# Attention: when ScalarE's and GpSimd's extra work is issued, and in what pieces

## The chip, the cores and the metric

One Trainium2 chip, one core of it. The metric is the device time of the whole program in microseconds (us). The kernel before took 2564.64 us (median of 3 runs, 2563.76 to 2566.25). The times below that name a place in the program are microseconds from the start of the span of one profiled execution.

## The reference

One layer of an encoder: 2048 tokens, width 1024, 16 heads of 64. The mixer has two kinds of heads. Eight are stick-breaking heads: for a query t, the weight of key s < t is sigmoid(z_s) times the product of (1 - sigmoid(z)) over the keys between s and t. Eight are chunk heads: a softmax over the own chunk of 64 keys and the 8 chunks before it, with a learned bias. The heads' outputs are joined, projected, and added to the input; a squared-ReLU MLP of width 4096 follows.

```python
log_beta = jax.nn.log_sigmoid(z)
log_1m_beta = jnp.where(strict, jax.nn.log_sigmoid(-z), 0.0)
suffix = lax.cumsum(log_1m_beta, axis=3, reverse=True) - log_1m_beta
w = jnp.where(strict, jnp.exp(log_beta + suffix), 0.0)
outs.append(jnp.einsum('bhqk,bkhd->bqhd', w.astype(v.dtype), vb))
```

All is float32. The kernel holds each float32 operand as a high and a low half and multiplies them in two or three matmuls.

## The kernel before

**Stages.** The projections fill the first 415 us, the attention 415 to 1262 us, the rest of the output projection and the MLP the time from there on. Each engine works through its instructions in the order in which the program issues them, so the order in which the code below calls `act`, `pool`, `dve` and `pe` is the order of the work. A helper records every operation, and that is why all compute rows of the trace carry the line L42; the rows are told apart by the names of their tiles.

**Units and steps.** The attention is cut into units: a head `h`, a group `g` of 512 queries (taken from the end of the sequence), and for a stick-breaking (SB) unit a block `c` of 512 keys. The units come in four runs: 24 SB units, 24 chunk (CA) units, 56 SB units, 8 CA units. Where one run ends and the next begins, the kind of heads changes; the text calls this a turn, and there are three. Each unit has 4 steps, so there are 448 steps in 847 us, 1.89 us each. The main loop does in step `i` the front half of unit step `i` and the back half of unit step `i - 8`:

- TensorE (PE) transposes the weights of the back unit into PSUM (tile `wt`);
- front half, `soft1` and `soft2`: for SB, ScalarE (ACT) takes the sigmoid of the scores `z`, VectorE (DVE) scans the products into `p`, GpSimd (POOL) copies one column of `p` and subtracts neighbours into the weights `b`; for CA, DVE adds the bias (`s`), ACT takes the exponential `e`, POOL divides (`e<-e,cols`);
- `parts`: ACT casts the high half of the transposed weights (`wth<-wt`), DVE subtracts the low half (`wtl<-wt,wth`);
- the jobs in `done`, which are the extra work;
- PE multiplies the weights with the values into the accumulator (`acc`), three `wt` tiles behind;
- PE computes the scores of the next step (`z`, or `cz` and `ct` for CA);
- `fill`: PE takes matmuls of the dense queue (tiles `pf`, `po`), as many as a credit allows. A dense row that ends sets `rest`, and `fill` then issues no dense work for that step.

The scores and the transposed weights share 4 PSUM buffers: `z`, `cz`, `ct` and `wt` of a step can be written only when DVE or ACT has read the tile that held the buffer. `acc` has 2 buffers.

**The extra work.** Jobs that one step puts in `soon` run in the next step's `done`, all of them. When a unit ends, `finish` copies the two 64-row halves of its accumulator on ACT (`otmp<-acc`, `o<-acc`) in one step. After the second head of a pair, `total` adds the two on POOL in the next step (`o<-o,otmp`, 128x512), and two steps on `keep` splits the sum: a cast on ACT (`os<-o`), a subtraction on POOL (`os<-o,os`), and a store to `scr_m`, from SP's queue. The RMS norm of finished rows runs beside this: ACT squares a row (`sq<-xr`), POOL adds it up (`r<-r,sq`, 128x512). A finished dense row of the projections also brings an ACT cast (`stf<-pf`, `svf<-pf`). At a turn, ACT loads another table for the new function, and does it by a 1-column activation (`cols<-zero`), before `parts`.

Of the kernel before, what the change touches and what calls it, by code (L numbers as in the profile page):

```python
# [9 lines left out]
F32 = mybir.dt.float32  # L10
F32R = mybir.dt.float32r
BF16 = mybir.dt.bfloat16
AF = mybir.ActivationFunctionType
# [66 lines left out]
def encoder_kernel(ctx, tc, xT, x3, wf, c, g1, g2, w_in, w_rest, gqk, bias, w_o, w1, w2, w_ada, b_ada, out):  # L80
# [670 lines left out]
    if True:  # L751
# [36 lines left out]
        def finish(u):  # L788
            r = (u.h % 2) * HD
            q = HD - r  # L790
            if u.h % 2 == 0:
                pend["o", u.g] = [op.tile([P, TB], F32, tag=t, name=f"{t}{u.nm}", bufs=3) for t in ("o", "otmp")]
            o, tmp = pend["o", u.g]
            act.copy(tmp[r : r + HD, :], u.acc[q : q + HD, :])
            act.copy(o[r : r + HD, :], u.acc[r : r + HD, :])
            if u.h % 2:
                soon.append(lambda: total(u, o, tmp))

        def total(u, o, tmp):

            pool.tensor_tensor(o, o, tmp, op=ALU.add)
            soon.append(lambda: soon.append(lambda: keep(u, o)))

        def keep(u, o):

            os = fp.tile([P, 2, TB], F32R, tag="st", name=f"os{u.nm}")
            split(os[:, 0, :], os[:, 1, :], o, pool)
            q = act if u is units[-1] else sp
            q.dma_start(scr_m[u.g, u.ca * 4 + u.h // 2], os.bitcast(F32))
            pairs[u.g] += 1  # L810
            if pairs[u.g] == KT and u.g > 0:
                filler.append(Filler(outproj, u.g))
# [4 lines left out]
        class Unit:  # L817
# [24 lines left out]

            def values(self, j):
                if j == 0 and self.first:
                    pend["acc"] = ppo.tile([P, TB], F32, tag="acc", name=f"acc{self.nm}")
                self.acc = pend["acc"]
                w = self.wt.pop(j)
                end = self.last and j == len(self.banks) - 1
                for m, (kb, q0, q1, at) in enumerate(self.banks[j]):
                    mine = slice(at * P, (at + q1 - q0) * P)  # L850
                    for l in range(2):
                        pe.matmul(
                            self.acc[:, q0 * P : q1 * P], self.v[kb // 4][:, kb % 4, :], w[l][:, mine],
                            start=self.first and j + m + l == 0, stop=end and l == 1 and m == len(self.banks[j]) - 1,
                        )
                if end:
                    soon.append(lambda: finish(self))

        DIAG = [[(3, 0, 4, 0)], [(2, 0, 3, 0), (0, 0, 1, 3)], [(1, 0, 2, 0)]]

# [313 lines left out]
        def finish_row(g, n, ps, xr):  # L1174

            residual(g, n, ps, xr)
            if g < 2 and drain:
                return
            stores.pop()()
            if g < 2:  # L1180
                return

            def square():
                sq = rows[g] if n == 0 else op.tile([P, TB], F32, tag="otmp", name=f"sq{g}_{n}", bufs=3)
                act.activation(sq, xr, AF.Square)
                if n:
                    soon.append(lambda: add(sq))

            def add(sq):
                pool.tensor_tensor(rows[g], rows[g], sq, op=ALU.add)  # L1190
                if n == KT - 1:
                    later.add(3, second)

            def second():
                pv = norm_sum(dense, rows[g], f"m{g}")

                def mean():
                    v = norm_mean(op, pv, f"m{g}")
                    y = op.tile([P, 4], F32, tag="ny", name=f"nym{g}")
                    rsqrt(y, v, op.tile([P, 4], F32, tag="nt", name=f"ntm{g}"))  # L1200
                    later.add(3, lambda: spread(y))

                later.add(2, mean)

            def spread(y):
                dg = norm_diag(op, y, f"m{g}")
                later.add(2, lambda: third(dg))
# [9 lines left out]
            soon.append(square)  # L1217

        LAG = 8
        STEPS = 4  # L1220
# [12 lines left out]
        credit = 0.0  # L1233
        rest = 0
        late, soon, first, second = [], [], [], []

        def fill(part, more=0):
# [31 lines left out]
        def load(u):  # L1269
            nonlocal kp1  # L1270
            if u.ca and u.g == 0 and u.h == 0:
                narrow.close()
                kp1 = narrow.enter_context(tc.tile_pool(name="kp2", bufs=3, side="right"))
            need = (10, 11) if u.ca else (2, 3, 0, 1) + ((4, 5) if u.g == 0 else ())
            if u.g < 2:
                while not all((p, u.g) in have for p in need):
                    later.flush()
                    for job in soon:
# [30 lines left out]
        for i in range(len(steps) + LAG):  # L1309
            if i % STEPS == 0:  # L1310
                if i // STEPS + AHEAD < len(units):
                    load(units[i // STEPS + AHEAD])
            vi = i - VST
            if vi >= 0 and vi % STEPS == 0 and vi // STEPS < len(units):
                units[vi // STEPS].load_values()
            front, fs = steps[i] if i < len(steps) else (None, 0)
            back, bs = steps[i - LAG] if i >= LAG else (None, 0)
            done = list(soon)
            soon.clear()
            js = []  # L1320
# [12 lines left out]
            if turned:  # L1333
                act.activation(cols[:, 1:2], zero, AF.Exp if front.ca else AF.Sigmoid)
            for j in js:
                back.parts(j)
                late.append((back, j))
            if turned:
                front.soft1(fs)
            if front is not None:  # L1340
                front.soft2(fs)
            for job in done:
                if turned:
                    later.add(3, job)
                else:
                    job()
            while len(late) > AVLAG:
                value(*late.pop(0))
            if i + 1 < len(steps):
                u, st = steps[i + 1]  # L1350
                u.scores(st)
            fill(front.weight if front else 0.6, 6 if turned else 0)
            if i + 1 < len(steps):
                u.behind(st)
            later.tick()
        for u, j in late:
            value(u, j)
        while soon:
            soon.pop(0)()
        later.flush()  # L1360
        while second:
            second.pop(0)()
    sp = osp
# [525 lines left out]
```

## Time and profile before

| what | value |
|---|---|
| median of 3 runs | 2564.64 us |
| the profiled execution | 2562.64 us |
| its span, first to last instruction | 2560.9 us |
| PE busy over the span | 2548.6 us |
| attention stage, 415 to 1262 us | 847.0 us |
| PE, PEld, DVE, ACT, POOL busy in that stage | 843.6, 742.2, 728.8, 604.6, 569.0 us |
| granted TensorE clock | 1.000 |

The profiled execution is 1.7 us longer than its span and 2.0 us shorter than the median of the runs. PE is TensorE's matmuls, and PEld is its weight loads, each of which runs ahead of its matmul. A row of the timeline reads: start, duration, engine, line, operation, out<-in, shape, count, and in brackets the idle time before it with what ended that idle time. In a list of waits, a row reads: engine and tile that waited, what it waited for, the us in total, how many times, and the longest.

### The profile page before, as it was taken

The page shows a single profiled execution, that of the slowest core. Times are in us where ns is not written, and L with a number is a line of the kernel's source. Part 1 is how long each engine was busy: PE and PEld are TensorE (multiplying, and loading weights), DVE is VectorE, ACT ScalarE, POOL GpSimd, SP SyncE. Part 2 cuts the span into 40 slices and gives each one's busy share as a digit, 9 for nine tenths or more (in the row PEclk, how much of TensorE's full clock was granted, in tenths as well). Part 3 has the DMA queues.
Part 4 walks back from the last instruction along what each step waited for, and adds up shares of the span by engine and source line. Part 5 has one row for each costly group of instructions (what it writes and reads, how often), then busy time and mean ns, then how long its engine had stood idle before and what let it go on. Part 6 is the DMA issues. An engine that isn't in the chain of part 4 may idle for free.

```text
span 2560.9 us, 39227 instructions
## 1 busy us (share of the span) xinstructions
PE 2548.6 (100%) x12851; PEld 2153.9 (84%) x12851; DVE 1866.3 (73%) x3102; ACT 1396.2 (55%) x2599; POOL 903.4 (35%) x1232
## 2 busy tenths in 40 slices
PE   9999999999999999999999999999999999999999
PEld 7888888889999988888888888888888888888887
DVE  7656767887779999998687787768756655555655
ACT  7323434778886666666654444656444444444443
POOL 4330244766667666776423333000003233100000
PEclk9999999999999999999999999999999999999999
DMA  9879887788888685757787777966773444465574
GB/s 396 337 282 373 314 325 253 247 270 269 252 254 271 214 268 196 239 187 226 249 335 259 256 264 277 338 225 218 255 247 135 154 154 144 164 241 192 202 272 151
DMA packets 251264, 633.90 MB, mean 248 GB/s; under 512 B 28210, under 2 KB 56882, under 8 KB 241203
## 3 DMA queue, kind: packets, MB, share of 16 engines
q1 hardware_dynamic: 249760, 626.67, 70.8%
q10 hardware_dynamic: 1298, 4.72, 0.5%
q8 instruction: 101, 1.65, 0.3%
q14 instruction: 105, 0.85, 0.1%
HBM read 439.92 MB, written 191.37 MB: 247 GB/s over the span
## 4 chain that ended last, share of the span: by engine, by line
PE 92%; DVE 3%; ACT 1%; DMA 1%; issue 1%; POOL 1%; SPq 0%; DVEq 0%; ACTq 0%; POOLq 0%
PE ps L42 46%; PE pt L42 11%; PE acc L42 7%; PE wt L42 7%; PE pf L42 6%; PE z L42 5%; PE po L42 4%; PE pq L42 3%; PE cz L42 2%; PE ct L42 1%; DVE p L42 1%; DVE h L42 1%; PE px L42 1%; POOL b L42 0%; DVE cy L42 0%
## 5 line engine op out<-in xcount | busy, mean ns | idle before, releaser
L42 PE MATMUL ps<-oph,opv 128*128 128x512 f32 x2688 | 611.9, 389 | 0.1
L42 PE MATMUL ps<-h,opw 128*128 128x512 f32 x2664 | 604.2, 389 | 0.0
L42 PEld LDWEIGHTS ps<-oph,opv 128*128 128x128 f32 x2688 | 503.9, 188 | 106.1 <-DVE opv L42 0.8
L42 PEld LDWEIGHTS ps<-h,opw 128*128 128x128 f32 x2664 | 500.0, 188 | 103.8
L42 POOL TENSOR_TENSOR b<-p 128x512 f32<-128x512 f32 (+1 forms) x320 | 292.4, 914 | 201.0 <-DVE p L42 121.5
L42 ACT CAST wth<-wt 128x512 fp32r<-128x512 f32 (+1 forms) x432 | 244.2, 567 | 167.2 <-PE wt L42 162.4
L42 DVE TENSOR_TENSOR wtl<-wt,wth 128x512 fp32r<-128x512 f32 (+1 forms) x432 | 279.9, 652 | 61.8 <-ACT wth L42 60.3
L42 DVE TENSOR_TENSOR oph<-hw,oph 128x512 fp32r<-128x512 f32 x224 | 156.1, 697 | 211.5 <-ACT oph L42 211.4
L42 ACT CAST oph<-hw 128x512 fp32r<-128x512 f32 x224 | 139.4, 622 | 274.9 <-PE ps L42 272.9
L42 PE MATMUL pt<-w,ht 128*128 128x512 f32 x1248 | 288.0, 391 | 0.0
L42 POOL TENSOR_TENSOR ts<-w 128x512 f32<-128x512 f32 x32 | 45.2, 1414 | 662.2 <-DMA w<-in_w_dram 516.8
L42 PEld LDWEIGHTS pt<-w,ht 128*128 128x128 f32 x1248 | 233.0, 188 | 47.5
L42 DVE TENSOR_TENSOR_SCAN p<-z,p,zero 128x512 f32<-128x512 f32 x192 | 245.5, 1280 | 30.8 <-ACT z L42 20.3
L42 PE MATMUL acc<-wth,v 128*128 128x512 f32 (+3 forms) x544 | 217.3, 404 | 0.0
L42 ACT ACTIVATE z<-z 128x512 f32<-128x512 f32 (+1 forms) x320 | 165.8, 520 | 61.9 <-PE z L42 58.0
L42 PE MATMUL z<-k,q 128*128 128x512 f32 (+3 forms) x640 | 183.5, 368 | 2.1 <-DVE p L42 1.7
L42 PE MATMUL acc<-wtl,v 128*128 128x512 f32 (+3 forms) x544 | 181.1, 347 | 0.0
L42 DVE TENSOR_TENSOR opw<-w,opw 128x512 fp32r<-128x512 f32 x127 | 96.4, 761 | 113.2 <-ACT opw L42 113.1
L42 POOL TENSOR_TENSOR e<-e,cols 128x640 f32<-128x640 f32 (+1 forms) x128 | 143.2, 1122 | 84.6 <-DVE cols L42 66.0
L42 PE MATMUL wt<-ident,b 128*128 128x128 f32 x1088 | 165.9, 272 | 0.7 <-DVE cols L42 0.3
L42 PE MATMUL po<-fx,ow 128*128 128x512 f32 x576 | 162.0, 393 | 0.0
L42 DVE TENSOR_TENSOR opv<-hw,opv 128x512 fp32r<-128x512 f32 x224 | 155.8, 695 | 0.0
(201 smaller groups left out, 4061.0 us busy)
## 6 DMA issues: line engine op xcount, KB each, us to landing
hw<-scr_hid SPq DMA_DIRECT2D x112, 512.0 KB, 3.8
q<-scr_q SPq DMA_DIRECT2D x128, 256.0 KB, 4.7
w<-in_w_dram SPq DMA_DIRECT2D x64, 512.0 KB, 5.4
hw<-scr_s SPq DMA_DIRECT2D x64, 512.0 KB, 4.6
fw<-scr_w SPq DMA_DIRECT2D x28, 1024.0 KB, 6.9
k<-scr_k SPq DMA_DIRECT2D x224, 128.0 KB, 4.2
v<-scr_v SPq DMA_DIRECT2D x112, 256.0 KB, 4.2
wa<-in_w_ada_dram SPq DMA_DIRECT2D x48, 512.0 KB, 7.7
```

Of the source, the lines that this page charges most:

```text
L42: return lambda *x, **y: self.tc.keep_in_program_order(f(*x, **y))
```

## The change

The extra work goes into two queues, `acts` for ACT and `pools` for POOL. At the end of a step's front half one job is taken from each; after a turn none is taken for that step and the two that follow; a step that has jobs in `done` takes none from `acts` unless an accumulator is waiting to be copied; in the last 8 steps, where no front unit is left, all are taken at once. An accumulator's second copy is put at the head of `acts` when the first is issued. The POOL additions and subtractions of 128x512 are cut in two of 128x256. The cast `os` comes 3 steps after the second half of its addition (1 in the last steps). A list `full` holds the units whose accumulators are not yet copied; before a new accumulator and before `parts`, copies are forced until at most one is left. The table load of a turn is issued one step earlier in the program. The stores to `scr_m` of the last steps go by ACT's queue. The norm's reciprocal root and its diagonal are cut over steps, and `fill` clears `rest` at a turn.

The first place is ACT's order where an SB unit ends shortly before the third turn (`otmp` and `o` are the two halves of its accumulator, `z` a sigmoid, `wth` a cast of `parts`, `sq` a square of the norm). Before:

```order
L42 CAST wth_7_0_1_0_15005<-wt_7_0_1_0_14994 128x512
L42 COPY otmp_6_0_3_15010<-acc_6_0_0_14599 64x512
L42 COPY o_6_0_3_15009<-acc_6_0_0_14599 64x512
L42 ACTIVATE z_7_0_3_1_15016<-z_7_0_3_1_15016 128x512
L42 CAST wth_7_0_1_1_15032<-wt_7_0_1_1_15021 128x512
L42 ACTIVATE z_7_0_3_2_15042<-z_7_0_3_2_15042 128x512
L42 CAST wth_7_0_1_2_15068<-wt_7_0_1_2_15057 128x512
L42 ACTIVATE sq_7_15072<-xr_7_14568 128x512
L42 ACTIVATE z_7_0_3_3_15076<-z_7_0_3_3_15076 128x512
L42 CAST wth_7_0_1_3_15101<-wt_7_0_1_3_15090 128x512
L42 ACT_TABLE_LOAD
```

Now:

```order
L42 CAST wth_7_0_1_0_15073<-wt_7_0_1_0_15062 128x512
L42 COPY otmp_6_0_3_15078<-acc_6_0_0_14661 64x512
L42 ACTIVATE z_7_0_3_1_15083<-z_7_0_3_1_15083 128x512
L42 CAST wth_7_0_1_1_15099<-wt_7_0_1_1_15088 128x512
L42 COPY o_6_0_3_15077<-acc_6_0_0_14661 64x512
L42 ACTIVATE z_7_0_3_2_15110<-z_7_0_3_2_15110 128x512
L42 CAST wth_7_0_1_2_15136<-wt_7_0_1_2_15125 128x512
L42 ACTIVATE sq_7_15140<-xr_7_14632 128x512
L42 ACTIVATE z_7_0_3_3_15144<-z_7_0_3_3_15144 128x512
L42 ACT_TABLE_LOAD
L42 ACTIVATE cols<-zero 128x1
L42 CAST wth_7_0_1_3_15170<-wt_7_0_1_3_15158 128x512
```

The second copy of the accumulator has moved behind one sigmoid and one cast, and the table load has moved ahead of one cast.

The second place is POOL's order around the end of the pair of heads 0 and 1 in the last query group of the second SB run (`b` is a weight, `p` its scan, `r` the sum of squares, `o` the pair's sum, `os` its low half). Before:

```order
L42 TENSOR_TENSOR r_11570<-r_11570,sq_6_12972 128x512
L42 TENSOR_TENSOR o_0_0_3_12569<-o_0_0_3_12569,otmp_0_0_3_12570 128x512
L42 COPY p_2_0_3_2_13020<-p_2_0_2_2_12903 128x1
L42 TENSOR_TENSOR b_2_0_3_2_13019<-p_2_0_3_2_13020 128x512
L42 COPY p_2_0_3_3_13042<-p_2_0_2_3_12921 128x1
L42 TENSOR_TENSOR b_2_0_3_3_13041<-p_2_0_3_3_13042 128x512
L42 TENSOR_TENSOR os_1_0_3_13051<-o_0_0_3_12569,os_1_0_3_13051 128x512
```

Now:

```order
L42 TENSOR_TENSOR r_11612<-r_11612,sq_6_13025 128x256
L42 COPY p_2_0_3_3_13095<-p_2_0_2_3_12974 128x1
L42 TENSOR_TENSOR b_2_0_3_3_13094<-p_2_0_3_3_13095 128x512
L42 TENSOR_TENSOR o_0_0_3_12621<-o_0_0_3_12621,otmp_0_0_3_12622 128x256
L42 COPY p_3_0_0_0_13122<-ones 128x1
L42 TENSOR_TENSOR b_3_0_0_0_13121<-p_3_0_0_0_13122 128x512
L42 TENSOR_TENSOR o_0_0_3_12621<-o_0_0_3_12621,otmp_0_0_3_12622 128x256
L42 COPY p_3_0_0_1_13145<-ones 128x1
L42 TENSOR_TENSOR b_3_0_0_1_13144<-p_3_0_0_1_13145 128x384
```

Two additions that stood one behind the other are now three of half the width (the fourth, the first half of `r`, stands further up) with a column copy and a weight between them; the subtraction `os` begins 7 rows after the last row shown.

PE's order differs in four pieces only, the matmuls of the norm's sums and of its spread for two row blocks (`pvm`, `prm`, 4 matmuls each), which now come later. No dense matmul, score, transpose or value matmul has another place. ScalarE has the same operations as before. GpSimd has 32 additions `o`, 32 subtractions `os` and 14 additions `r` as halves.

The diff, cut to what the prediction speaks of:

```diff
         def finish(u):
...
-            act.copy(tmp[r : r + HD, :], u.acc[q : q + HD, :])
-            act.copy(o[r : r + HD, :], u.acc[r : r + HD, :])
-            if u.h % 2:
-                soon.append(lambda: total(u, o, tmp))
-
-        def total(u, o, tmp):
-
-            pool.tensor_tensor(o, o, tmp, op=ALU.add)
-            soon.append(lambda: soon.append(lambda: keep(u, o)))
...
+            def first():
...
+                act.copy(tmp[r : r + HD, :], u.acc[q : q + HD, :])
+                acts.insert(0, lambda: whole(o, tmp))
+
+            acts.append(first)
+            full.append(u)
+
+            def whole(o, tmp):
+                act.copy(o[r : r + HD, :], u.acc[r : r + HD, :])
+                full.pop()
+                if u.h % 2:
+                    halves(o, o, tmp, ALU.add, lambda: later.add(3 if front is not None else 1, lambda: acts.append(lambda: high(u, o))))
+
+        def halves(out, a, b, op, end):
+
+            def half(n):
+                c = slice(n * TB // 2, (n + 1) * TB // 2)
+                pool.tensor_tensor(out[:, c], a[:, c], b[:, c], op=op)
+                if n:
+                    end()
+
+            for n in range(2):
+                pools.append(lambda n=n: half(n))
+
+        def high(u, o):
             os = fp.tile([P, 2, TB], F32R, tag="st", name=f"os{u.nm}")
-            split(os[:, 0, :], os[:, 1, :], o, pool)
-            q = act if u is units[-1] else sp
+            act.copy(os[:, 0, :], o)
+            halves(os[:, 1, :], o, os[:, 0, :].bitcast(F32), ALU.subtract, lambda: keep(u, os))
+
+        def keep(u, os):
+            q = act if front is None or u is units[-1] else sp
             q.dma_start(scr_m[u.g, u.ca * 4 + u.h // 2], os.bitcast(F32))
...
             def values(self, j):
                 if j == 0 and self.first:
+                    while len(full) > 1:
+                        acts.pop(0)()
...
-            rest = max(0, rest - 1)
+            rest = 0 if more else max(0, rest - 1)
...
-            if turned:
-                act.activation(cols[:, 1:2], zero, AF.Exp if front.ca else AF.Sigmoid)
+            turns = front is not None and i + 1 < len(steps) and front.ca != steps[i + 1][0].ca
+            if turns and not front.ca:
+                act.activation(cols[:, 1:2], zero, AF.Exp)
+            while len(full) > 1:
+                acts.pop(0)()
...
+            if turns and front.ca:
+                act.activation(cols[:, 1:2], zero, AF.Sigmoid)
...
+            hold = 3 if turned else max(0, hold - 1)
+            if not hold:
+                for q in (pools, acts):
+                    n = 1 if front is not None else len(q)
+                    if q is acts and done and not full:
+                        n -= 1
+                    for _ in range(min(n, len(q))):
+                        q.pop(0)()
```

More of the change, by code (lines that the diff above doesn't have):

```diff
@@ L790, in finish @@
             q = HD - r
-            if u.h % 2 == 0:
-                pend["o", u.g] = [op.tile([P, TB], F32, tag=t, name=f"{t}{u.nm}", bufs=3) for t in ("o", "otmp")]
-            o, tmp = pend["o", u.g]
-            act.copy(tmp[r : r + HD, :], u.acc[q : q + HD, :])
-            act.copy(o[r : r + HD, :], u.acc[r : r + HD, :])
-            if u.h % 2:
-                soon.append(lambda: total(u, o, tmp))
-        def total(u, o, tmp):
-            pool.tensor_tensor(o, o, tmp, op=ALU.add)
-            soon.append(lambda: soon.append(lambda: keep(u, o)))
-        def keep(u, o):
+            def first():
+                if u.h % 2 == 0:
+                    pend["o", u.g] = [op.tile([P, TB], F32, tag=t, name=f"{t}{u.nm}", bufs=3) for t in ("o", "otmp")]
+                o, tmp = pend["o", u.g]
+                act.copy(tmp[r : r + HD, :], u.acc[q : q + HD, :])
[16 more added lines that the diff above has]
+        def high(u, o):
             os = fp.tile([P, 2, TB], F32R, tag="st", name=f"os{u.nm}")
-            split(os[:, 0, :], os[:, 1, :], o, pool)
-            q = act if u is units[-1] else sp
+            act.copy(os[:, 0, :], o)
+            halves(os[:, 1, :], o, os[:, 0, :].bitcast(F32), ALU.subtract, lambda: keep(u, os))
+        def keep(u, os):
+            q = act if front is None or u is units[-1] else sp
             q.dma_start(scr_m[u.g, u.ca * 4 + u.h // 2], os.bitcast(F32))
@@ L856, in values @@
                 if end:
-                    soon.append(lambda: finish(self))
+                    finish(self)
         DIAG = [[(3, 0, 4, 0)], [(2, 0, 3, 0), (0, 0, 1, 3)], [(1, 0, 2, 0)]]
@@ L1186, in square, with summed @@
                 if n:
-                    soon.append(lambda: add(sq))
-            def add(sq):
-                pool.tensor_tensor(rows[g], rows[g], sq, op=ALU.add)
+                    halves(rows[g], rows[g], sq, ALU.add, summed)
+            def summed():
                 if n == KT - 1:
@@ L1199, in mean, with polish, half @@
                     y = op.tile([P, 4], F32, tag="ny", name=f"nym{g}")
-                    rsqrt(y, v, op.tile([P, 4], F32, tag="nt", name=f"ntm{g}"))
-                    later.add(3, lambda: spread(y))
+                    pool.tensor_tensor(y, v, mhalf[:, :4], op=ALU.pow)
+                    later.add(1, lambda: polish(y, v))
                 later.add(2, mean)
-            def spread(y):
-                dg = norm_diag(op, y, f"m{g}")
-                later.add(2, lambda: third(dg))
+            def polish(y, v):
+                t = op.tile([P, 4], F32, tag="nt", name=f"ntm{g}")
+                pool.tensor_tensor(t, y, y, op=ALU.mult)
+                pool.tensor_tensor(t, t, v, op=ALU.mult)
+                pool.tensor_scalar(t, t, -0.5, 1.5, op0=ALU.mult, op1=ALU.add)
+                pool.tensor_tensor(y, y, t, op=ALU.mult)
+                later.add(2, lambda: spread(y))
+            def spread(y):
+                dg = op.tile([P, 4, P], F32, tag="ndg", name=f"ndgm{g}", bufs=1)
+                def half(a):
+                    dve.tensor_tensor(
+                        dg[:, a : a + 2], ident.unsqueeze(1).to_broadcast([P, 2, P]),
+                        y[:, a : a + 2].unsqueeze(2).to_broadcast([P, 2, P]), op=ALU.mult,
+                    )
+                half(0)
+                later.add(1, lambda: half(2))
+                later.add(3, lambda: third(dg))
             def third(dg):
@@ L1216, in finish_row @@
                 rows[g] = rp.tile([P, TB], F32, tag="r", name=f"r{g}")
-            soon.append(square)
+            acts.append(square)
         LAG = 8
@@ L1235, in encoder_kernel @@
         late, soon, first, second = [], [], [], []
+        acts, pools, full = [], [], []
+        hold = 0
         def fill(part, more=0):
@@ L1277, in load @@
                     later.flush()
+                    while pools:
+                        pools.pop(0)()
                     for job in soon:
@@ L1357, in encoder_kernel @@
             value(u, j)
-        while soon:
-            soon.pop(0)()
-        later.flush()
+        while soon or acts or pools or later.jobs:
+            for jobs in (soon, acts, pools):
+                while jobs:
+                    jobs.pop(0)()
+            later.flush()
         while second:
```

## The prediction

> **What bounds the kernel now.** I read the page's busy shares first, then the busy times of each stage of the attention, then what the weight loads waited for, and last the timeline around those waits.
>
> ```profile
> span 2560.9 us, 39227 instructions
> PE 2548.6 (100%) x12851; PEld 2153.9 (84%) x12851; DVE 1866.3 (73%) x3102; ACT 1396.2 (55%) x2599; POOL 903.4 (35%) x1232
> ```
>
> TensorE is busy for 2548.6 of 2560.9 us. Since the change removes no matmul, it can only gain from gaps between matmuls. Busy time by stage, in the columns PE, PEld, DVE, ACT, POOL, and behind them the granted clock, which is full (1.00):
>
> ```profile
> 566.00:770.00 204.00, 203.94 (x1314) 184.00 (x1313) 158.49 (x528) 172.43 (x378) 135.74 (x130) 1.00 0.85 262
> 900.00:1190.00 290.00, 288.65 (x1595) 241.34 (x1594) 263.26 (x333) 184.46 (x339) 197.91 (x328) 1.00 0.69 222
> sum 847.00, PE 843.56 PEld 742.20 DVE 728.82 ACT 604.58 POOL 568.99; mean PE 168.71 PEld 148.44 DVE 145.76 ACT 120.92 POOL 113.80
> ```
>
> The first CA run (566 to 770 us) keeps ACT busy for 172.43/204 = 85%; the second SB run (900 to 1190 us) keeps DVE at 263.26/290 = 91%. Neither has room for much extra work in one step. What the weight loads (PEld) waited for from 415 to 1190 us:
>
> ```profile
> PEld z L42 <- DVE p L42: 5.8, 13, 0.8
> PEld wt L42 <- DVE wtl L42: 2.9, 10, 0.6
> PEld ct L42 <- DVE wtl L42: 1.0, 1, 1.0
> PEld wt L42 <- DVE cols L42: 0.5, 1, 0.5
> PEld wt L42 <- POOL b L42: 0.2, 1, 0.2
> ```
>
> That is 5.8 + 2.9 + 1.0 + 0.5 + 0.2 = 10.4 us in 26 waits, the whole stock that the change can draw on. Two parts of it have nothing to do with a unit's end: the start (415 to 425 us), and the first turn, whose rows are the ones with `ct` and `cols` above (1.0 + 0.5 = 1.5 us).
>
> ```profile
> PEld z L42 <- DVE p L42: 1.1, 2, 0.6
> PEld wt L42 <- POOL b L42: 0.2, 1, 0.2
> ```
>
> The start takes 1.1 + 0.2 = 1.3 us. Left are 10.4 - 1.5 - 1.3 = 7.6 us in 26 - 5 = 21 waits. The same list for the second SB run, and below the "..." for the first CA run, has as its main rows:
>
> ```profile
> PEld z L42 <- DVE p L42: 3.8, 8, 0.8
> ...
> PEld wt L42 <- DVE wtl L42: 1.5, 6, 0.3
> ```
>
> Half of it, 3.8 us, is `z` waiting for a scan in the second SB run, and the largest of these waits is this one:
>
> ```profile
> 1171.29 0.58 ACT L42 COPY otmp<-acc 64x512 f32<-64x512 f32 x1
> 1171.89 0.58 ACT L42 COPY o<-acc 64x512 f32<-64x512 f32 x1
> 1172.37 0.58 ACT L42 ACTIVATE z<-z 128x512 f32<-128x512 f32 x1
> 1173.39 1.28 DVE L42 TENSOR_TENSOR_SCAN p<-z,p,zero 128x512 f32<-128x512 f32 x1 [0.97 <-POOL p L42]
> 1173.65 0.36 PE L42 MATMUL acc<-wth,v 128*128 128x256 f32 x1
> 1173.86 0.28 PE L42 MATMUL acc<-wtl,v 128*128 128x256 f32 x1
> 1174.73 0.30 PEld L42 LDWEIGHTS z<-k,q 128*128 128x128 f32 x2 [0.80 <-DVE p L42]
> ```
>
> Both copies of a finished accumulator stand ahead of one sigmoid, so the sigmoid ends at 1172.37 + 0.58 = 1172.95. The scan waits (0.97 us), though the list names POOL's column copy as the last releaser, and the next scores wait 0.80 us for the scan to free their PSUM buffer. The other form:
>
> ```profile
> 1023.61 1.28 POOL L42 TENSOR_TENSOR r<-r,sq 128x512 f32<-128x512 f32 x1
> 1024.85 1.29 POOL L42 TENSOR_TENSOR o<-o,otmp 128x512 f32<-128x512 f32 x1
> 1026.17 0.62 ACT L42 CAST os<-o 128x512 fp32r<-128x512 f32 x1 [1.37 <-POOL o L42]
> ...
> 1027.66 0.48 PE L42 MATMUL acc<-wth,v 128*128 128x512 f32 x1
> 1027.97 0.40 PE L42 MATMUL acc<-wtl,v 128*128 128x512 f32 x1
> ...
> 1028.66 0.30 PEld L42 LDWEIGHTS z<-k,q 128*128 128x128 f32 x2 [0.72 <-DVE p L42]
> ```
>
> Two additions stand one behind the other on POOL, ACT blocks 1.37 us on the sum, the sigmoid queued behind the cast is late, and PE's scores wait 0.72 us.
>
> **What a wait costs.** In the first case the last matmul before the wait and the first after it start 1174.73 - 1173.86 = 0.87 us apart, against 1173.86 - 1173.65 = 0.21 for the pass before: 0.66 lost of a wait of 0.80. In the second it is 0.69 against 0.31: 0.38 of 0.72. One wait thus costs 0.53 to 0.83 of its length by this count, and a little more where the pass itself needs less than the pair's spacing. I take 0.75: 7.6 x 0.75 = 5.7 us of the end hang on the ends of units.
>
> **The change part by part.**
>
> *One job a step (removes).* By the new order the second copy stands one sigmoid and one cast later, and the cast `os` at least three steps behind its addition. In the second SB run ACT is busy 184.46/290 = 64% of a step of 847/448 = 1.89 us, which leaves 0.68 us: one copy of 0.58 fits, two (1.16) do not. So a wait with nothing but the two copies behind it should go, as should those behind a blocked `os`. By my reading of the timeline around the 21 waits, about 60% of their time is of these two forms, about 27% has a cast of a dense tile in the same step, and the rest stands behind a square that waited for its row. The rule that a step with dense jobs gives no ACT job does not hold while an accumulator waits, so the second kind keeps half; the third keeps two thirds. These fractions are my estimate: 0.9 x 60% + 0.5 x 27% + 0.33 x 13% = 72%, and 5.7 x 0.72 = 4.1 us go. From the other side, all 7.6 us could go; below nothing, the waits could double (a rival).
>
> *Halves on POOL (adds).*
>
> ```profile
> L42 POOL TENSOR_TENSOR o<-o,otmp 128x512 f32<-128x512 f32 x32 | 41.3, 1290 | 8.2 <-ACT o L42 8.2
> L42 POOL TENSOR_TENSOR b<-p 128x512 f32<-128x512 f32 x222 | 231.3, 1042 | 151.8 <-DVE p L42 89.6 <-PE z L42 25.3 <-PE wt L42 23.7
> L42 POOL TENSOR_TENSOR b<-p 128x256 f32<-128x256 f32 x31 | 19.1, 615 | 6.8 <-PE wt L42 3.4 <-DVE p L42 1.9
> ```
>
> A weight of half the width takes 615 ns and not 521, so each cut adds 2 x 615 - 1042 = 188 ns; 32 + 32 + 14 = 78 cuts add 14.7 us of POOL time. POOL is busy 569 of 847 us and waits for DVE most of its idle time, so this lies in its idle time: 0. What stood ahead of a column copy and a weight was up to 1.28 + 1.29 = 2.57 us and is now one half, 1.29/2 + 0.09 = 0.74 us.
>
> *Accumulators handed back later (adds).* PE's first value matmul of a new unit can wait for the second copy, which is now up to one step later. The tight place is the middle group of each CA head:
>
> ```profile
> 631.03 0.19 ACT L42 ACTIVATION_READ_ACCUMULATOR e<-s,cols 128x1 f32 x1
> 632.25 0.48 PE L42 MATMUL acc<-wth,v 128*128 128x512 f32 x1
> ```
>
> The copy now stands behind this row (631.22); with its 0.58 us it ends at 631.80, 0.45 before PE needs it. ACT is full there, so the work ahead of it is no longer than before, and the margin holds unless ACT slips by half a microsecond. At the second turn I count 0.2 us of margin. I put 0.2 us on this place; the bounds are 0 and one copy in each of 8 heads, 8 x 0.58 = 4.6 us.
>
> *Table load earlier (moves).* Rows around the first turn:
>
> ```profile
> 558.55 0.26 ACT L42 ACTIVATE z<-z 128x128 f32<-128x128 f32 x1
> 559.35 0.38 ACT L42 CAST wth<-wt 128x256 fp32r<-128x256 f32 x1 [0.53 <-PE wt L42]
> 559.74 1.28 ACT L42 ACT_TABLE_LOAD   x1
> 561.03 0.20 ACT L42 ACTIVATE cols<-zero 128x1 f32<-128x1 f32 x1
> ...
> 561.29 0.42 PEld L42 LDWEIGHTS cz<-k,q 128*128 128x128 f32 x2
> 561.31 0.59 ACT L42 CAST wth<-wt 128x512 fp32r<-128x512 f32 x1
> ```
>
> The load now starts behind the sigmoid, 558.81, and with the column ends at 558.81 + 1.28 + 0.20 = 560.29. The cast (0.38) and the low half behind it, taken as long as the cast's own 0.38 to 0.42, end at 561.09, and PE loads the scores that take this buffer at 561.29. A margin of 0.2 covers it: 0. Nothing is gained either: the cast that this turn's `ct` waits for began at 561.31, 0.08 us after ACT was free (561.23), so it was not the load that held it. The Trainium skill ("ScalarE: Activation LUTs", section "What ACT_TABLE_LOAD costs") adds to the load of 1283 ns a drain of about 1380 ns. The rows here show the load's length, 1.28 us, but no drain: the column starts 0.01 us after the load. If the drain came with the new place, the cast would be 1.38 us later and the scores 1.2 us late at this turn, an estimate from that page.
>
> *No dense rest at a turn.* PE's order shows no dense matmul moved. At the first turn the row that ends there sets the rest again inside the same call. This part does nothing: 0.
>
> *The tail.* After the last unit the sum, the cast and the subtraction run one behind the other on the way to the last store, and the halves add 2 x 0.19 = 0.38 us. What waits for it, after 1262 us:
>
> ```profile
> PEld pso L42 <- DMA opm<-scr_m: 0.3, 1, 0.3
> ```
>
> This load is late already, so up to 0.38 us show; I take 0.3. The extra stores on ACT's queue wait for POOL when ACT has little else to do: 0.
>
> **Sum.** -4.1 + 0.2 + 0.3 = -3.6 us, 2562.64 - 3.6 = 2559.0 for the profiled execution. It stands 2.0 us under the median of the runs, so the forecast for the median is 2564.64 - 3.6 = 2561.0 us. A difference below about 0.2%, 5.1 us, can't be told from none here, and the forecast lies within it.
>
> **The rivals.**
>
> *The ends of units cost their full waits, and all go.* For it: a load that waits has nothing ahead of it, and one copy fits in the free 0.68 us. Against it: the dense casts and squares stay where they are. 7.6 us go, nothing is added: 2564.64 - 7.6 = 2557.0 us.
>
> *The waits only move.* For it: in the SB run DVE has 9% free, and a sigmoid that is 0.58 late in two steps is as late in sum as one that is 1.16 late. Then PE loses about the same: -0.5 to +0.5, near 2564.5 us. Against it: the free 0.68 us.
>
> *Each unit's end disturbs two steps (slower).* If a step has no room even for one copy, both steps lose what one lost, and 5.7 us are added, with the 0.5 above: 2570.8 us. The place is where ACT is at 85%, the first CA run, and the SB run at DVE's 91%; it decides once a step's free time on ACT is under 0.58 us. In the CA run it is 0.15 x 1.89 = 0.28, which speaks for it; that only 1.5 of the 7.6 us are lost there with both copies in one step speaks against it.
>
> *The table load delays its cast by a further drain.* The place is the two turns from SB to CA. If a second load's time hung on the new place, 1.28 - 0.2 (the margin) = 1.1 us would show at each: 2561.0 + 2.2 = 2563.2 us. That no idle time follows the load here speaks against it. By the page's figure it would be 2561.0 + 2 x 1.2 = 2563.4 us, an estimate.
>
> **How the numbers follow.** The forecast's own case 0.47 (2558.8 to 2563), all waits gone 0.22, waits only moved 0.17, two steps disturbed 0.09, the drain 0.05. Faster by over 0.2% is below 2559.5: the 0.22 and about a quarter of the forecast's case, 0.34. Slower by over 0.2% is the 0.09 and 0.02 for what I haven't seen, 0.11. Within 0.2% is the rest, 0.55. The range reaches down to the case of all waits gone, 2556.5, and up past the case of moved waits to half of the doubled ones, 2566.5.
>
> **What would show it.** Right: the list of weight-load waits from 415 to 1190 us falls from 10.4 to near 5 us, the 8 waits of `z` in the second SB run to 2 or 3 short ones, the turn keeps its 1.5 us, and POOL's busy time rises by 14.7 us. Wrong: waits of `acc` for ACT's `o` in the first CA run (late accumulators), waits of `z` that stay at 3.8 us but stand two to a unit's end, a new wait of `cz` at a turn, or gaps in the MLP, which the change doesn't touch.

## The result, and the profile after

The changed kernel took 2562.02 us (median of 21 runs), the kernel before beside it 2564.70 us (21 runs). The ratio is 0.9986, with a 95% interval of 0.9980 to 0.9992: 3.6 us less, between 2.1 and 5.1. The two medians by themselves lie 2.7 us apart. The forecast for the median was 2561.0, 3.6 us less. The profiled execution has this page:

```profile
span 2557.5 us, 39336 instructions
PE 2545.4 (100%) x12851; PEld 2153.0 (84%) x12851; DVE 1875.1 (73%) x3104; ACT 1394.5 (55%) x2599; POOL 915.0 (36%) x1310
```

The span is 3.4 us shorter, and so is PE's busy time (3.2 us); ACT has as much work as before, and POOL 11.6 us more. What the weight loads waited for from 415 to 1190 us, the list that read 10.4 us before:

```profile
PEld z L42 <- DVE p L42: 2.4, 4, 1.1
PEld ct L42 <- DVE wtl L42: 1.7, 3, 1.0
PEld wt L42 <- issue: 0.6, 2, 0.4
PEld pvm L42 <- POOL e L42: 0.6, 1, 0.6
PEld wt L42 <- DVE cols L42: 0.5, 1, 0.5
PEld wt L42 <- POOL b L42: 0.2, 1, 0.2
PEld wt L42 <- DVE wtl L42: 0.2, 1, 0.2
```

It reads 6.2 us now. The start (1.3 us) and the first turn (1.5 us) are in it unchanged. Of the 7.6 us that hung on the ends of units, 1.5 us are left or have moved to a neighbour: 0.7 of `ct`, 0.6 of `wt` with "issue", for which the profile shows no releaser, and 0.2 of `wt` for `wtl`. New are 1.3 us of `z` in two waits (at 1054.93 and 1057.56 us, 0.28 and 1.06 us), and `pvm`, 0.6 us. At the unit's end that cost 0.80 us before, ACT and DVE now read (first ACT, below the "..." DVE):

```profile
1168.28 0.58 ACT L42 ACTIVATE z<-z 128x512 f32<-128x512 f32 x1
1168.88 0.58 ACT L42 CAST wth<-wt 128x512 fp32r<-128x512 f32 x1
1169.36 0.58 ACT L42 COPY o<-acc 64x512 f32<-64x512 f32 x1
1169.87 0.58 ACT L42 ACTIVATE z<-z 128x512 f32<-128x512 f32 x1
...
1168.94 1.28 DVE L42 TENSOR_TENSOR_SCAN p<-z,p,zero 128x512 f32<-128x512 f32 x1 [0.31 <-ACT z L42]
1171.38 1.28 DVE L42 TENSOR_TENSOR_SCAN p<-z,p,zero 128x512 f32<-128x512 f32 x1
```

One copy stands between a cast and a sigmoid. The scan behind the first copy waits 0.31 us instead of 0.97, the next one not at all, and PE waits for neither. The new waits of `z` have another origin, shown with the fifth experiment. In the tail (1262 to 1340 us) the list is

```profile
PEld ps L42 <- DVE opr L42: 1.7, 1, 1.7
PEld pso L42 <- DMA opm<-scr_m: 0.5, 1, 0.5
```

against 1.5 and 0.3 us before. The 0.4 us more can't be laid to the change: in a second profile of the changed kernel the two read 0.9 and 1.5 us.

### The profile page after: what moved, and what is told of

Same layout as the page of the kernel before. It is cut to its first block, busy times and chain, and to the rows that moved or that the text cites. A ratio compares the mean times of both kernels' runs of the same rounds, so it can differ in the third digit from the quotient of the medians.

```text
span 2557.5 us, 39336 instructions
## 1 busy us (share of the span) xinstructions
PE 2545.4 (100%) x12851; PEld 2153.0 (84%) x12851; DVE 1875.1 (73%) x3104; ACT 1394.5 (55%) x2599; POOL 915.0 (36%) x1310
## 4 chain that ended last, share of the span: by engine, by line
PE 92%; DVE 3%; ACT 1%; DMA 1%; issue 1%; POOL 1%; SPq 0%; DVEq 0%; POOLq 0%; ACTq 0%
PE ps L42 46%; PE pt L42 11%; PE acc L42 7%; PE wt L42 7%; PE pf L42 6%; PE z L42 5%; PE po L42 4%; PE pq L42 3%; PE cz L42 2%; PE ct L42 1%; DVE h L42 1%; PE px L42 1%; DVE opv L42 0%; DVE ty L42 0%; DVE cy L42 0%
```

## The experiments

Theory: the two copies of a finished accumulator in one step are too much beside the step's own ACT work, and one copy a step fits. Rivals: the gain comes from the later cast `os` or from the halves on POOL; or each step with a copy loses something, so that the copies only spread the loss.

**1. Both copies in one step again** (undoes one part of the change).

```diff
-                acts.insert(0, lambda: whole(o, tmp))
+                whole(o, tmp)
```

> The changed kernel, but with both copies of an accumulator in one step again; halves, later casts and everything else stay. If two copies in one step are what does not fit beside a step's own ACT work (theory), the waits of the weight loads from 415 to 1190 us go from 7.2 us (changed kernel) back to about 10 us, with waits of z and wt right behind the pairs of copies, and the time comes to about 2564.5 us (ratio to before 0.9995 to 1.0005). If the gain came from the halves on POOL and the later cast (rival), the waits stay under 8 us and the ratio stays near 0.9986.

Measured: 2565.19 us (10 runs), ratio to before 1.0004 (0.9995 to 1.0013). Its list of waits from 415 to 1190 us sums to 10.5 us, with these at the head:

```profile
PEld z L42 <- DVE p L42: 4.3, 8, 1.1
PEld wt L42 <- DVE wtl L42: 3.0, 10, 0.7
PEld pf L42 <- DMA fw<-scr_w: 1.3, 1, 1.3
```

The gain in time is gone, though the halves, the later cast and the earlier table load are all still in. The list is not the old one, though. Some 4.4 us stand at the ends of units, against 7.6 before: `wt` is back in full, while the two waits of `z` behind a blocked `os` in the second SB run (0.72 and 0.50 us before) did not come back, for the cast is still held back. In their place 1.8 us stand behind the halves of the diagonal, and 1.3 us is PE waiting for weights of the dense queue, a wait that has nothing to do with the copies and reads 0 and 1.0 us in the two profiles of the changed kernel. So the other parts do take out some waits; with what they add, they bring no time that this run could show.

**2. The split of the copies alone** (in the kernel before; nothing else of the change).

```diff
-            act.copy(o[r : r + HD, :], u.acc[r : r + HD, :])
-            if u.h % 2:
-                soon.append(lambda: total(u, o, tmp))
+            def whole():
+                act.copy(o[r : r + HD, :], u.acc[r : r + HD, :])
+                if u.h % 2:
+                    soon.append(lambda: total(u, o, tmp))
+
+            soon.append(whole)
```

> The kernel before with one edit: the second copy of an accumulator goes one step later. Theory: two copies in one step are the main cause, so this alone brings most of the gain: the waits of the weight loads from 415 to 1190 us fall from 10.4 to about 7 us (z from 5.8 to under 3.5; the waits behind a blocked os stay), ratio 0.9985 to 0.9995. Rival (the gain needs the later cast os or the halves too): the list stays at 9 us or more, ratio 0.9995 or above.

Measured: 2559.99 us (11 runs), before 2564.09, ratio 0.9982 (0.9973 to 0.9991). The list sums to 5.7 us, with these at the head:

```profile
PEld z L42 <- DVE p L42: 2.7, 7, 0.6
PEld ct L42 <- DVE wtl L42: 1.9, 3, 1.0
```

ACT's own waits from 415 to 1262 us have for `os`

```profile
ACT os L42 <- POOL o L42: 0.9, 2, 0.7
```

One edit brings as much as the whole change (the two intervals overlap), somewhat more than I expected of it. It moves more than the copy: the second copy calls for the addition, so the addition and the cast `os` of each pair come one step later too, still two steps apart. In the kernel before that row read

```profile
ACT os L42 <- POOL o L42: 4.8, 9, 1.4
```

so most of the blocking went as well, though the cast was not held back any further. Whether the lighter step or the new place of the addition did that isn't shown: in experiment 1, with both copies in one step and the cast held back, ACT's `os` waits only 0.3 us. For the time, experiments 1 and 2 together settle the cause: without the split the gain is gone, and the split, with the delay of the addition that it brings, is enough.

**3. A third copy in the same step** (the kernel before, with the first copy issued twice).

```diff
+            act.copy(tmp[r : r + HD, :], u.acc[q : q + HD, :])
             act.copy(tmp[r : r + HD, :], u.acc[q : q + HD, :])
```

> The kernel before, with the first copy of every accumulator issued twice, so three ACT copies (1.75 us) stand in one step. Theory: a step of 1.89 us has about 0.7 us free on ACT in the second SB run, so each of the 64 unit ends loses up to 0.58 us more; half of them do: 64 x 0.58 x 0.3 to 0.5, about 10 us more (5 to 18), ratio 1.002 to 1.007, and the waits of z on DVE's scan grow from 5.8 us to over 10. Rival (the waits have another cause, or ACT has room): under 2 us more, waits of z under 7 us.

Measured: 2585.51 us (4 runs), ratio 1.0082 (1.0067 to 1.0097), 21 us more. The list from 415 to 1190 us sums to 28.1 us, and its two main rows are

```profile
PEld z L42 <- DVE p L42: 15.9, 29, 1.0
PEld wt L42 <- DVE wtl L42: 7.6, 12, 0.9
```

The direction is the theory's, the size above my range: 64 copies of 0.58 us are 37 us of ACT work, and more than half of it came out at the end. In the first CA run `wt` alone rose to 5.9 us, so a third copy finds no room there either.

**4. The same third copy as a job of its own** (the changed kernel, in a third step).

```diff
-                acts.insert(0, lambda: whole(o, tmp))
+                acts.insert(0, lambda: again(o, tmp))
+
+            def again(o, tmp):
+                act.copy(tmp[r : r + HD, :], u.acc[q : q + HD, :])
+                acts.insert(0, lambda: whole(o, tmp))
```

> The changed kernel with the same third copy, dealt out as a job of its own in a third step (the accumulator is free one step later). Theory (one copy fits in a step): the waits of z and wt stay within 2 us of the changed kernel's (2.4 and 0.8 us), ratio 0.998 to 0.9995; the later accumulator may show as waits of acc on ACT's o in the first CA run, up to 8 x 0.9 us. Rival (every step with an extra copy loses): half as much again as the copies cost before, 3 us or more of waits of z and wt, spread over the third steps, ratio 1.000 or above.

Measured: 2574.36 us (5 runs), ratio 1.0040 (1.0026 to 1.0054), so the time lies outside what the theory expected. But the waits are not the rival's:

```profile
PEld acc L42 <- ACT o L42: 9.6, 12, 1.5
PEld po L42 <- DVE xr L42: 2.6, 1, 2.6
PEld z L42 <- DVE p L42: 1.3, 3, 0.6
```

Of the waits of `z`, 1.1 us are the start's, and no other is longer than 0.3 us; `wt` waits for DVE's `wtl` nowhere. Three steps with one copy each cost the scan next to nothing: one copy does fit. The price is the other mechanism of the prediction. The accumulator comes free one step later, and PE's first value matmul of a new unit waits for it 12 times, 11 of them in the first CA run, where the margin was estimated at 0.45 us. I had put up to 8 x 0.9 = 7.2 us on it and not counted it in the ratio. The 2.6 us of `po` was not expected, and its cause stays open.

**5. The diagonal of the norm in one operation** (undoes a part of the change that the forecast had not priced).

```diff
-                half(0)
-                later.add(1, lambda: half(2))
+                dve.tensor_tensor(
+                    dg, ident.unsqueeze(1).to_broadcast([P, 4, P]),
+                    y.unsqueeze(2).to_broadcast([P, 4, P]), op=ALU.mult,
+                )
                 later.add(3, lambda: third(dg))
```

> The changed kernel with the norm's diagonal in one DVE operation of 128x512 again. In the changed kernel the two halves took 1.00 and 0.99 us, each ending 0.28 us after a multiplication on POOL ended, and behind them the scores of head 4 waited 1.1 us, the longest wait left. Theory (each half waits on DVE for a POOL operation to end): one operation waits once at most and takes 0.6 to 1.5 us, the wait of z falls to 0.3 or less, and the list of z from 2.4 to about 1.3 us. Rival (the wait comes from the square and the other norm work at that place): the wait of z stays at 0.8 us or more.

In the changed kernel the halves stand like this, and the wait of `z` of 1.1 us follows at 1057.56:

```profile
1052.36 1.04 POOL L42 TENSOR_TENSOR b<-p 128x512 f32<-128x512 f32 x1 [0.78 <-PE wt L42]
1052.69 1.00 DVE L42 TENSOR_TENSOR ndgm<-ident,nym 128x256 f32<-128x256 f32 x1
1053.35 0.38 POOL L42 COPY p<-p 128x1 f32<-128x1 f32 x1
...
1055.05 1.04 POOL L42 TENSOR_TENSOR b<-p 128x512 f32<-128x512 f32 x1 [1.32 <-DVE p L42]
1055.38 0.99 DVE L42 TENSOR_TENSOR ndgm<-ident,nym 128x256 f32<-128x256 f32 x1
1056.04 0.38 POOL L42 COPY p<-ones 128x1 f32<-128x1 f32 x1
...
1057.56 0.30 PEld L42 LDWEIGHTS z<-k,q 128*128 128x128 f32 x2 [1.06 <-DVE p L42]
```

Each half ends 0.28 to 0.29 us (1053.69 and 1056.37) after POOL's multiplication ended (1053.40 and 1056.09), and each column copy of POOL beside it takes 0.38 us instead of its usual 0.19. In these rows the two engines take turns. In the kernel before the one operation for this block read

```profile
1054.34 0.68 DVE L42 TENSOR_TENSOR ndgm<-ident,nym 128x512 f32<-128x512 f32 x1
```

0.68 us, against 1.99 us for the two halves, on an engine that is busy 91% of this stretch. With one operation again in the changed kernel:

```profile
1052.79 1.04 POOL L42 TENSOR_TENSOR b<-p 128x512 f32<-128x512 f32 x1 [0.78 <-PE wt L42]
1053.12 1.26 DVE L42 TENSOR_TENSOR ndgm<-ident,nym 128x512 f32<-128x512 f32 x1
```

It takes 1.26 us, having met POOL once, and the list from 415 to 1190 us has `z` at 1.9 us with 0.6 us as its longest; in the second SB run the longest wait fell from 1.1 to 0.5 us. The theory's direction holds, and the saving is 0.5 us rather than the 1.0 I wrote down. Experiment 6, where the halves of the diagonal stay, shows the same link: there the first half began just as POOL's weight ended (1052.52), and kept 0.41 us.

```profile
1052.47 0.41 DVE L42 TENSOR_TENSOR ndgm<-ident,nym 128x256 f32<-128x256 f32 x1
1054.58 1.00 DVE L42 TENSOR_TENSOR ndgm<-ident,nym 128x256 f32<-128x256 f32 x1
```

One half is stretched there and not two, and the wait of `z` behind them is 0.62 us. The one run of experiment 5 took 2565.13 us, but PE's first MLP matmul waited 4.3 us in it, which has to do with another place (the last section).

**6. Whole additions and subtractions on POOL** (one job a step kept).

```diff
-            for n in range(2):
-                pools.append(lambda n=n: half(n))
+            pools.append(lambda: half(0))
```

> The changed kernel with GpSimd's additions and subtractions whole again (128x512), still one job a step. Theory: the halves are worth nothing to the end, because POOL waits for DVE in most of its idle time and the weights are needed 8 steps later: waits of z, wt and ct on DVE from 415 to 1190 us stay within 1 us of the changed kernel's 4.8 us, POOL's busy time falls by 14 us, and the wait of pso for opm falls from 0.5 to about 0.3. Rival: one whole addition (1.29 us) beside a step's weight does not fit on POOL either; waits of z grow by 1.5 us or more.

Measured in its one run: 2562.20 us. The list sums to 5.7 us, with `z` at

```profile
PEld z L42 <- DVE p L42: 1.7, 3, 0.6
```

`z`, `ct` and `wt` are no worse than with halves, and no gain of the halves shows. `pso`'s wait for `opm` stayed at 0.5 us, so the tail's 0.2 us isn't the halves' either; experiment 2, which has nothing of the change in the tail, reads 0.5 us as well.

**7. The cast `os` not held back behind its addition.**

```diff
-                    halves(o, o, tmp, ALU.add, lambda: later.add(3 if front is not None else 1, lambda: acts.append(lambda: high(u, o))))
+                    halves(o, o, tmp, ALU.add, lambda: acts.append(lambda: high(u, o)))
```

> The changed kernel with the cast os not held back 3 steps behind its addition. Theory: ACT blocks on POOL's sum again, as in the kernel before (4.8 us in 9 waits), which is a second source of late sigmoids: ACT's os waits 3 us or more for POOL's o, and the waits of z and wt grow by 1 to 2 us. Rival: only the pairs of copies matter; waits of z and wt stay within 0.5 us of the changed kernel's, whatever os waits.

Measured in its one run: 2584.99 us. I expected 1 to 2 us more of waits of `z` and `wt`; the waits of `z` alone grew by 15.6 us. I had compared it with the kernel before, where the cast stands two steps behind the addition. Here POOL's second half and ACT's cast fall into one step, and ACT has to wait for all that stands ahead of the half on POOL. ACT's waits, and then the weight loads':

```profile
ACT os L42 <- POOL o L42: 29.7, 19, 2.8
```

```profile
PEld z L42 <- DVE p L42: 18.0, 20, 2.8
```

With 29.7 us of blocked ACT come 18.0 us of waits of `z`. With the queues of the changed kernel the holding back is necessary; it is a repair of what the queues would do, and no gain over the kernel before.

**8. The table load at its old place.**

```diff
-            if turns and not front.ca:
-                act.activation(cols[:, 1:2], zero, AF.Exp)
+            if turned:
+                act.activation(cols[:, 1:2], zero, AF.Exp if front.ca else AF.Sigmoid)
...
-            if turns and front.ca:
-                act.activation(cols[:, 1:2], zero, AF.Sigmoid)
```

> The changed kernel with the table load of a turn back at its old place. Theory: no difference; the first turn keeps its waits of ct (1.0 us) and cols (0.5 us), and there are no others within 10 us of the three turns. Rival (the earlier load hid something): 0.5 us or more of new waits of z, wt or cz at a turn.

Measured in its one run: 2562.28 us. The first turn kept its waits in both kernels (`ct` 1.0 us, `cols` 0.5 us), and no wait of `z`, `wt` or `cz` appeared at a turn. Nothing that the move saves or costs shows in this run.

**9. The changed kernel again, and mended versions.** Again, on the same chip as the next:

> The changed kernel once more, for a comparison on the same chip with the next: ratio to before 0.998 to 0.9992, waits of the weight loads from 415 to 1190 us 7.2 us as in its first profile, within 0.5.

Measured: 2563.58 us (11 runs), ratio 0.9987 (0.9978 to 0.9997). The list from 415 to 1190 us sums to 6.7 us; the 7.2 us in the expectation was my slip for 6.2.

With one diagonal, and whole sums in the last steps only:

> The changed kernel with the norm's diagonal in one operation and, in the last steps, whole additions and subtractions on POOL. Theory: 1.0 us less wait of z in the second SB run and 0.2 to 0.3 us less in the tail, so about 1.3 us less than the changed kernel (ratio to before 0.9978 to 0.9988); the list of waits from 415 to 1190 us falls from 7.2 to about 6 us and pso's wait for opm to 0.3 us. Rival: the tail's wait hangs on other transfers and stays at 0.5 us or more.

Measured: 2560.78 us (11 runs), ratio 0.9985 (0.9976 to 0.9994). The list fell to 5.6 us, but `pso` waited 1.1 us for `opm` in its profile, so for the tail the rival's figure came: the wait is not shorter with whole sums. That other transfers hold it is not shown. The ratio is within 0.0002 of the changed kernel's beside it, so no gain over it is shown.

With one diagonal and whole sums everywhere:

> The changed kernel with whole additions and subtractions on POOL everywhere and the diagonal in one DVE operation. Theory (halves are worth nothing; the split diagonal costs 1 us): waits from 415 to 1190 us of 6 us or less, POOL's busy time back near 903 us, ratio 0.9975 to 0.9988. Rival (whole operations push column copies and weights late): waits of z 1.5 us or more above the 1.8 us of the kernel with halves and a whole diagonal.

Measured: 2559.66 us (11 runs) against 2564.09, ratio 0.9979 (0.9970 to 0.9988). The list sums to 5.2 us, POOL is back at 903.3 us. This is the lowest ratio of all, but its interval overlaps those of the changed kernel and of experiment 2, so it isn't shown to be faster than either.

The same with POOL's first sums of the MLP held until DVE's operands are done:

```diff
-steps[KT].fetch() if n + LEFT == KT else None
+steps[KT].load() if n + LEFT == KT else None
...
+                if self.mb and self.j == 0:
+                    pool.tensor_copy(s1[:, 0:1], hops[4, 3][:, 1, 0:1].bitcast(F32))
                 column_sum(pool, s1, d["21"], d["22"], ALU.add)
```

> The kernel with whole operations and whole diagonal, and in the MLP's first weights one more edit: POOL's first four sums wait for the last low half of DVE's right operands (a copy of one column put ahead of them). The changed kernel's 11 runs lay in two groups, 2559.6 to 2560.5 and 2563.6 to 2567.7, and in its two profiles, which differ by 8.5 us, PE's first MLP matmul waited 0 and 3.8 us, with DVE's squares and halves stretched from 0.68 to 1.78 us wherever POOL's sums ran beside them. Theory (that meeting makes the upper group): no run in an upper group, spread under 2.5 us, the squares all 0.7 us; the sums start later, so PE's wait for opr may grow by up to 1.5 us; median at or under that of the kernel without this edit. Rival (the upper group has another source): two groups as before, spread of 4 us or more.

Measured: 2560.39 us (11 runs), ratio 0.9984 (0.9976 to 0.9993), spread 3.8 us. The kernel without this edit showed no upper group in that comparison either (spread 3.3 us), and its median is 0.7 us lower, so the run doesn't tell the theory from its rival.

Not tried alone were the forced copies ahead of a new accumulator, the three steps without jobs after a turn, the reciprocal root in two steps and the stores on ACT's queue. Experiment 2 has none of them and is not slower than the change.

The variation between runs lies partly outside the attention. So here is the length of the attention stage alone in each profile, from the start of the first matmul of `wt` to the start of the last of `acc` (415.99 to 1265.32 us in the kernel before):

| profile | attention stage, us |
|---|---|
| before | 849.3 |
| changed, first and second profile | 845.4, 846.4 |
| 1, both copies in one step | 850.0 |
| 2, split alone, in the kernel before | 845.3 |
| 3, third copy in the same step, in the kernel before | 868.8 |
| 4, third copy in a step of its own | 858.8 |
| 5, one diagonal | 844.7 |
| 6, whole sums | 845.7 |
| 7, cast not held back | 869.8 |
| 8, table load at its old place | 845.7 |

The two profiles of the changed kernel differ by 0.9 us, so differences of that size decide nothing. Experiments 5, 6 and 8 are within it of the changed kernel; 1, 3, 4 and 7 are not, and 2 is where the whole change is.

## Why the prediction was right

*The sum.* -3.6 us predicted, -3.6 us by the ratio, within -2.1 and -5.1. The mechanism is the predicted one: the ends of units, and ACT's two copies in one step. That the number fits this well is luck, for two terms are wrong in opposite directions.

*The stock.* The list of 10.4 us, less the start and the first turn, was the right place to look: the changed kernel leaves both untouched, and 6.1 of the other 7.6 us are gone, 80% where I put 72%. The shares of 60%, 27% and 13% that the 72% was made of were not measured one by one.

*The price of a wait* was too low. I took 0.75 us of the end for 1 us of waiting. By the stage lengths above, the change took out 4.2 us of waits and 3.9 us of the stage. Experiment 1 put back 4.3 us of waits up to 1190 us and 0.8 behind it, and 4.5 us of the stage; experiment 3 added 17.7 us and 1.1 behind it, and 19.5 us of the stage. By these three a wait costs 0.88 to 1.04 of its length. Why the two waits that I worked the price out from gave 0.53 and 0.83 stays open.

*What was missing* is 1.9 us of new waits: 1.3 us behind the halved diagonal and 0.6 us of `pvm`, whose place in PE's order I had shown to move and had not priced. 6.1 - 1.9 = 4.2 us of waits go, nearly the 4.1 us of time that I had summed from a lower price and no new waits.

*The tail* (0.3 us predicted, for the halves on POOL): `pso`'s wait grew by 0.2 us, but it does so without the halves too (experiments 2 and 6). No run supports this term. From the last value matmul to the end the changed kernel's first profile is 0.6 us longer than that of the kernel before; what of it is the change's isn't shown.

*Accumulators handed back later* (0.2 us predicted): no wait of `acc` in the changed kernel. Experiment 4 shows the mechanism is real and one step away, 9.6 us.

*Halves on POOL:* 2 x 737 ns for 1290 ns, 184 ns a cut where I had worked out 188. The halves add 13.9 us by their own rows, 14.7 predicted, and POOL's total over the program rose by 11.6. No cost and no worth showed at the end (experiment 6). *Table load:* no cost and no gain showed (experiment 8). The drain that the Trainium skill ("ScalarE: Activation LUTs", section "What ACT_TABLE_LOAD costs") adds behind a load did not show as a wait of `cz` at the turn.

*The rivals.* "All go" had the price of a wait nearly right, and its share, 100% where 80% went, too high. "The waits only move" fell with the list, which lost 4.2 us, and with experiment 4, where even three copies in three steps left the scan's waits smaller; the same experiment speaks against "two steps disturbed". The drain fell with the table load. The dense rest moves nothing in PE's order, as the prediction had it.

## What to carry to other kernels

Where one engine has a little room in each step, what matters of a burst is how many of its jobs fall into one step: here two copies of 0.58 us against some 0.68 us of room cost about 4.6 us in total, and moving one of them by one step, with the addition behind it, brought that much. Look at what such a split does at the other end: each step of delay comes off the margin of whoever waits for the buffer, and a job that is queued right behind its producer on another engine blocks everything behind it. And after an edit list that moves many things, try its single parts: one of some eight carried the gain.

## What the runs showed that I had not expected

In some rows DVE and POOL hold each other up. The diagonal's halves above are one case; the other lies at the start of the MLP, where two executions of one and the same kernel differ. In the second profile of the changed kernel (span 2566.0 us, 8.5 us longer than the first), POOL's sums of the first MLP weights begin while DVE works on a tile in PSUM, `pso` (DVE's and POOL's rows alone):

```profile
1324.68 0.68 DVE L42 TENSOR_TENSOR cy<-cy,cy 128x512 f32<-128x512 f32 x1
1325.28 0.74 DVE L42 SCALAR_TENSOR_TENSOR cxr<-pso,mod,cxr 128x512 f32<-128x512 f32 x1
1325.52 1.29 POOL L42 TENSOR_TENSOR ts<-w 128x512 f32<-128x512 f32 x1 [56.86 <-PE pso L42]
1325.94 1.41 DVE L42 TENSOR_TENSOR h<-cy,h 128x512 fp32r<-128x512 f32 x1
1326.89 1.62 POOL L42 TENSOR_TENSOR ts<-ts,w 128x512 f32<-128x512 f32 x1
1327.28 1.78 DVE L42 TENSOR_TENSOR cy<-cy,cy 128x512 f32<-128x512 f32 x1
1328.47 1.74 POOL L42 TENSOR_TENSOR w<-w 128x512 f32<-128x512 f32 x1
1328.98 1.78 DVE L42 TENSOR_TENSOR h<-cy,h 128x512 fp32r<-128x512 f32 x1
1330.18 1.71 POOL L42 TENSOR_TENSOR ts<-w,ts 128x512 f32<-128x512 f32 x1
1330.68 1.75 DVE L42 TENSOR_TENSOR cy<-cy,cy 128x512 f32<-128x512 f32 x1
```

The weight loads' list for that stretch has

```profile
PEld ps L42 <- issue: 3.8, 1, 3.8
```

From there the engines alternate, DVE's 0.68 us become 1.41 to 1.78 us for four operations in a row, and PE's first MLP matmul comes 3.8 us late, for a wait whose releaser the profile does not name. In the first profile POOL came in the middle of one of DVE's `h`, found DVE busy back to back, and was the one to wait:

```profile
1322.61 0.68 DVE L42 TENSOR_TENSOR h<-cy,h 128x512 fp32r<-128x512 f32 x1
1322.91 3.94 POOL L42 TENSOR_TENSOR ts<-w 128x512 f32<-128x512 f32 x1 [56.34 <-DMA w<-in_w_dram]
```

DVE kept its 0.68 us up to the last `h`, which took 1.61, and there was no such wait of PE. The Trainium skill ("SBUF — State Buffer", section "SBUF: two separate sides") says that the two engines share a pair of ports under an exclusive lock, that whichever starts first holds it for its whole instruction and the other blocks, and that this concerns DVE operations in a two-port mode, or with two inputs in SBUF against a GpSimd operation that reads SBUF. The durations here agree: the diagonal, the squares and the halves of `h` have both inputs in SBUF and stretch, while the scans, which read `z` from PSUM, keep their 1.28 us, and `cxr`, which reads `pso` from PSUM, its 0.74.

Fourteen profiles were taken for this case. Four stretched DVE operations in a row ahead of the first MLP matmul stand in two of them, this one and that of experiment 5, and in these two alone that matmul waits without a releaser, 3.8 and 4.3 us; in the others at most one operation is stretched there. So the two go together. That DVE's lateness is what PE waits for fits the order of the rows, but the profile does not name it. It would account for some 4 of the 8.5 us between the two profiles of the changed kernel; the rest is spread over the projections, the attention and the MLP. The attempt to take the meeting away (experiment 9) told nothing about the other executions, and that stays open.
